# Attention value products: from two split operands over 128 columns to float32, two heads in the halves of the columns

## The chip, the cores and the metric

The kernel runs on one core of one Trainium2 chip. The metric is device time in microseconds for one execution, the median of several runs. Five engines work side by side: TensorE (PE; its weight loads are listed as PEld), VectorE (DVE), ScalarE (ACT), GpSimd (POOL) and SyncE (SP), whose queue issues the DMAs.

## The reference, cut to what matters

One layer of a hybrid encoder: 2064 tokens (16 meta tokens and 2048 others) of width 1024. After a projection, 8 heads of width 64 do stick-breaking attention over causal key prefixes, a recurrent branch (RG-LRU) runs beside it, an output projection and a gated FFN with a causal convolution follow. What the change touches is the attention:

```
for blk in range(t_len // Q_BLOCK):            # 128 queries
    z = einsum("bhqd,bhkd->bhqk", qb, kb) * scale
    mask = s_pos < t_pos
    log_keep = where(mask, log_sigmoid(-z), 0.0)
    after = cumsum(log_keep, reverse=True) - log_keep
    w = where(mask, exp(log_sigmoid(z) + after), 0.0)
    out = einsum("bhqk,bhkd->bhqd", w, vb)
```

The kernel uses the same thing in another form. With S the product of sigmoid(-z) from a key to the end, a weight is a difference of two neighbouring S, so the output is the last value plus a sum of S times the differences of neighbouring value rows.

## The kernel before, in words

The kernel works in stages. First come the norm, the projections and the recurrent branch (to some 580 us), then attention, then the output projection with the second norm (from some 1126 us), then the FFN. Products that must be as exact as float32 are made from operands in a shorter format (float32r): an operand is split into a high part H (a cast) and a low part L (the rest), and H·H, H·L and L·H are added.

Attention goes by head (8) and, within a head, by groups g of two query blocks of 128 (8 groups, and g = -1 for the meta tokens), in the order 3, 7, -1, 0, 6, 1, 5, 2, 4. There are 72 such units. The products of one unit are issued ahead of the outputs of the unit before it (`late`). The order on each engine is then set by a planner that simulates the program and issues by its own costs; the trace shows what it chose.

`load_head` (lines 115 to 144) brings a head's keys (`K2`: H and L in the two halves of the partitions) and two shifted copies of its values; GpSimd subtracts them (line 136) and splits the difference into H and L (lines 92, 93), which lie side by side in `dv`, 64 + 64 columns. Two sets of these buffers alternate between heads. `load_q` (line 548) brings the queries of a unit, four buffers.

`products_of` (555): for one query block, a float32r matmul with the queries' H and one with their L for each chunk of up to 512 keys (569, 570), the sigmoid on ScalarE (571), then a scan on VectorE backwards over the keys (578 for the first chunk with the mask, 580 for two chunks at a time). The result `kp` has 128 queries by all keys of the prefix.

`outputs_of` (616) transposes `kp` by 128x128 blocks on TensorE (helper on line 97) into a PSUM bank of 512 columns, that is two key blocks by two query blocks. When a bank is full, `flush` (600) empties it: ScalarE casts it to float32r (`tH`, line 585, by turns into the tiles `qk` and `tH`), VectorE subtracts (`tL`, 586), and for each key block two matmuls run (612), with all 128 columns of `dv` as the stationary operand and the 256 columns of `tH` and then `tL` as the moving one. So all four partial products H·H, H·L, L·H, L·L are formed; the two halves of the accumulator's partitions hold those with the high and those with the low part of `dv`. There is one accumulator bank `v`. `store_o` (588) adds the last value as a bias on ScalarE (594), and stores both halves apart (596). The output projection's `mix` (521) loads both and adds them on VectorE (526), and loads the recurrent branch.

Of the kernel before, what the change touches and what calls it, by code (L numbers as in the profile page):

```python
# [16 lines left out]
P = 128  # L17
# [21 lines left out]
def f(ap):  # L39
    return ap.bitcast(F32)  # L40
# [15 lines left out]
def hymba_block(  # L56
# [22 lines left out]
    od = {g: dram.tile([2, 4, P, META if g < 0 else 2 * P], F32, name=f"od{g + 1}") for g in range(-1, NT // 2)}  # L79
# [32 lines left out]
    heads = {}  # L112
    hb_stack = ExitStack()

    def load_head(hd, hb):
        j, hh = hd // 2, hd % 2
        rows = slice(hh * HD, hh * HD + HD)
        K2 = hb.tile([P, T], F32R, name="K2", tag="K2")
        dv = hb.tile([P, NT + 1, 2, HD], F32R, name="dv", tag="dv")
        nc.gpsimd.memset(f(dv[:, NT]), 0.0)  # L120
        cuts = [0, 4, 8, NT]
        for s0, s1 in zip(cuts, cuts[1:]):
            c0 = s0 * P + (META if s0 else 0)
            c1 = s1 * P + META
            for e in range(2):
                nc.sync.dma_start(f(K2[e * HD:(e + 1) * HD, c0:c1]), kd[j][e, rows, c0:c1])
            va = hb.tile([P, 9, HD], F32, name="va", tag="va")
            vb = hb.tile([P, 9, HD], F32, name="vb", tag="vb")
            m = s1 - s0
            for v, o in ((va, 1), (vb, 0)):  # L130
                nc.sync.dma_start(v[:, :m], vd[j][o + s0 * P:o + s1 * P, hh].rearrange("(s p) d -> p s d", p=P))
                if s1 == NT:
                    nc.sync.dma_start(v[:META, m], vd[j][o + NT * P:o + T, hh])
            parts = [(P, u, u + 4) for u in range(0, m, 4)] + ([(META, m, m + 1)] if s1 == NT else [])
# [4 lines left out]
        vl = hb.tile([NT + 1, HD], F32, name="vl", tag="vl")  # L139
        nc.sync.dma_start(vl[0:1], vd[j][META:META + 1, hh])  # L140
        nc.sync.dma_start(vl[1:], vd[j][META + P:1 + T:P, hh])
        vlT = hb.tile([P, NT + 1], F32, name="vlT", tag="vlT")
        nc.gpsimd.memset(vlT[HD:], 0.0)
        return j, rows, K2, dv, vlT, vl

# [23 lines left out]
    with ExitStack() as A:  # L169
# [332 lines left out]
        def before(j, i):  # L502
            if j == 2 and i == 0:
                heads[0] = load_head(0, hbE)
# [16 lines left out]
    def mix(mH, mL, src, t0, n):  # L521

        g, c0 = (-1, 0) if t0 < META else divmod(t0 - META, 2 * P)
# [3 lines left out]
        for ks, m in ((slice(0, 4), src[0]), (slice(4, 8), src[2])):  # L527
            nc.scalar.copy(mH[:, ks], m)
            nc.vector.tensor_tensor(mL[:, ks], m, f(mH[:, ks]), op=ALU.subtract)
# [4 lines left out]
    with ExitStack() as B:  # L534
# [10 lines left out]
        G = 2  # L545
        LOW = META + 8 * P

        def load_q(head, t0, n):
            j, rows = head[:2]
            q2 = hq.tile([P, 2, G * P], F32R, name="q2", tag="q2", bufs=4)  # L550
            for e in range(2):
                nc.sync.dma_start(f(q2[e * HD:(e + 1) * HD, :, :n]), qd[j][:, rows, t0:t0 + n].rearrange("s d t -> d s t"))
            return q2

        def products_of(head, i, q2, qc):

            K2 = head[2]
# [8 lines left out]
            for ci, sz in enumerate(sizes):  # L566
                c0 = hi - sz if ci == 0 else c0 - sz
                zt = acc_bank()
                nc.tensor.matmul(zt[:rn, :sz], lhsT=q2[:, 0, qc:qc + rn], rhs=K2[:, c0:c0 + sz], start=True, stop=False)  # L569
                nc.tensor.matmul(zt[:rn, :sz], lhsT=q2[:, 1, qc:qc + rn], rhs=K2[:, c0:c0 + sz], start=False, stop=True)  # L570
# [13 lines left out]
        def evac(h, l, src):  # L584
            nc.scalar.copy(h, src)
            nc.vector.tensor_tensor(l, src, f(h), op=ALU.subtract)  # L586

        def store_o(head, av, i0, t0, m):
            j, rows, vlT = head[0], head[1], head[4]
            ov = a1.tile([P, G * P], F32, name="qn", tag="qn", bufs=2)  # L590
            for c in range(0, m, P):
                e = min(c + P, m)
                b = i0 + 1 + c // P
                nc.scalar.activation(ov[:, c:e], av[:, c:e], AF.Identity, bias=vlT[:, b:b + 1])
            for a in range(2):
                nc.sync.dma_start(od[i0 // G][a, j, rows, :m], ov[a * HD:(a + 1) * HD, :m])

        nflush = [0]

        def flush(head, av, pend, cols, pt, nj):  # L600
            dv = head[3]
            nflush[0] += 1
            if nflush[0] % 2:
                tH = a1.tile([P, 2, 256], F32R, name="qk", tag="qk", bufs=2).rearrange("p a t -> p (a t)")
            else:
                tH = wk.tile([P, 512], F32R, name="tH", tag="tH", bufs=2)
            tL = wk.tile([P, 512], F32R, name="tL", tag="tL", bufs=4)
            pp = pend[0][2]
# [7 lines left out]
        def outputs_of(head, g, kps):  # L616
            if g < 0:
                pt = tu_bank()
                transpose(pt[:META, :META], kps[0][:META, :META])
                av = pmv.tile([P, 2, 256], F32, name="v", tag="v")[:, 0]  # L620
                flush(head, av, [(0, 0, META, 0, META)], META, pt, 1)
                store_o(head, av, -1, 0, META)
                return
            i0 = g * G
            av = pmv.tile([P, 2, 256], F32, name="v", tag="v")[:, 0]
            nj = i0 + G + 1
            pend, cols = [], 0
            pt = tu_bank()
            for s in range(nj):
                first = max(0, s - 1 - i0)  # L630
                nn = (G - first) * P
                if cols + nn > 512:
                    flush(head, av, pend, cols, pt, nj)
                    pt = tu_bank()
                    pend, cols = [], 0
                for b in range(first, G):
                    c = cols + (b - first) * P
                    transpose(pt[:, c:c + P], kps[b][:, s * P:(s + 1) * P])
                pend.append((s, first * P, P, cols, nn))
                cols += nn  # L640
            flush(head, av, pend, cols, pt, nj)
            store_o(head, av, i0, META + i0 * P, G * P)

        def make_products(head, g):
            if g < 0:
                return [products_of(head, -1, load_q(head, 0, META), 0)]
            q2 = load_q(head, META + g * G * P, G * P)
            return [products_of(head, g * G + b, q2, b * P) for b in range(G)]
# [3 lines left out]


        def finish_head(head):

            vlT, vl = head[4:]
            pt = tu_bank()
            transpose(pt[:HD, :NT + 1], vl)
            nc.vector.tensor_copy(vlT[:HD], pt[:HD, :NT + 1])

        units = [(hd, g) for hd in range(HEADS) for g in (3, 7, -1, 0, 6, 1, 5, 2, 4)]
        late = []
        seen = set()
        for n, (hd, g) in enumerate(units):
            if hd not in heads:
                heads[hd] = load_head(hd, (hbE, hbO)[hd % 2])
            if hd not in seen:
                seen.add(hd)
                finish_head(heads[hd])
            if late:  # L670
                outputs_of(*late.pop(0))
            kps = make_products(heads[hd], g)
            late.append((heads[hd], g, kps))
# [17 lines left out]
        tabs = [staging(), staging(), wl.tile([P, LOW + 112], F32, name="kp", tag="kp", bufs=4)[:, :512]]  # L691
# [41 lines left out]
    with ExitStack() as CD:  # L733
# [24 lines left out]
        with ExitStack() as C:  # L758
# [8 lines left out]
            def mixed(i):  # L767
                src = [cp.tile([P, 4, P], F32, name=f"m{a}", tag=f"m{a}", bufs=1) for a in range(3)]
                mix(*(mA, mB)[i % 2], src, META + (i - 1) * P, P)
# [244 lines left out]
```

## Time and profile before

| | us |
|---|---|
| three runs | 2718.18, 2722.47, 2722.88 |
| median | 2722.47 |
| the profiled execution | 2722.01 |
| its span in the trace | 2720.3 |
| TensorE busy | 2563.3 (94%) |
| VectorE busy | 1802.9 (66%) |
| ScalarE busy | 1241.5 (46%) |
| GpSimd busy | 1185.4 (44%) |

All trace numbers come from one profiled execution. The trace's times run from the start of its span. A busy TensorE is no sign that it is at its peak: its products overlap, and their ends are modelled. A share over the whole span mixes stages with different limits, so the views below are taken by stretch.

### The profile page before, as it was taken

Reading aid. Unit: us, or ns where it says so; the run is one execution under the profiler, and the core shown is the slowest. Engines: PE = TensorE matmul, PEld = TensorE weight load, DVE = VectorE, ACT = ScalarE, POOL = GpSimd, SP = SyncE. Lnnn points to the kernel's source line nnn. Section 1 sums busy time; section 2 is a strip of 40 time slices with the busy share of each in tenths; the row PEclk is TensorE's granted clock in tenths of the full one; section 3 lists DMA queues with packets and bytes.
Section 4 is the critical chain, followed back from the end, with each engine's and each line's share of the span. In section 5 each row is a group of like instructions: output and inputs, shape, how many; then the busy total and the mean of one; then the engine's idle time right before and its main releaser. Section 6 shows DMA issues by size and latency. Waiting matters only on the chain. (4 is left out here: it accounts for less than half of the span.)

```text
span 2720.3 us, 40399 instructions
## 1 busy us (share of the span) xinstructions
PE 2563.3 (94%) x15012; PEld 2293.5 (84%) x15012; DVE 1802.9 (66%) x2080; ACT 1241.5 (46%) x2331; POOL 1185.4 (44%) x1152
## 2 busy tenths in 40 slices
PE   7998889988888888999899999999999999999999
PEld 6998889977777778788799999988788888887887
DVE  5678853259999999655677667553745666665443
ACT  4355532246666666432355454432434545453221
POOL 4455564434522321000265555534456665653443
PEclk9999989999999999999899999999999999999999
DMA  5311143243333321577322222244653222225463
GB/s 157 111 33 33 45 113 98 76 113 96 102 81 85 83 78 50 138 222 223 108 86 71 91 74 78 86 159 146 208 169 109 79 84 79 85 79 172 141 211 109
DMA packets 316860, 296.41 MB, mean 109 GB/s; under 512 B 62182, under 2 KB 269270, under 8 KB 316662
## 3 DMA queue, kind: packets, MB, share of 16 engines
q1 hardware_dynamic: 316662, 293.82, 35.5%
q8 instruction: 118, 1.93, 0.3%
q14 instruction: 80, 0.66, 0.1%
HBM read 211.68 MB, written 82.07 MB: 108 GB/s over the span
## 5 line engine op out<-in xcount | busy, mean ns | idle before, releaser
L876 PE MATMUL bk<-mb,wt 128*128 128x258 f32 (+2 forms) x5544 | 878.8, 321 | 11.5 <-ACT u L906 2.3
L876 PEld LDWEIGHTS bk<-mb,wt 128*128 128x128 f32 x5544 | 794.9, 190 | 95.4 <-DVE c L910 3.2
L705 POOL TENSOR_TENSOR wt<-wst,wt 128x512 fp32r<-128x512 f32 (+1 forms) x264 | 485.5, 1845 | 488.8 <-ACT wt L704 263.6
L705 DVE TENSOR_TENSOR wt<-t,wt 128x512 fp32r<-128x512 f32 x88 | 173.4, 1973 | 213.0 <-ACT wt L704 213.0
L108 PE MATMUL bk<-wt 128*128 128x512 f32 x704 | 276.4, 394 | 8.0 <-ACT wt L704 8.0
L109 PE MATMUL bk<-wt 128*128 128x512 f32 x704 | 276.6, 393 | 0.0
L110 PE MATMUL bk<-wt 128*128 128x512 f32 x704 | 271.9, 391 | 4.2 <-DVE wt L705 4.2
L704 ACT CAST wt<-wst 128x512 fp32r<-128x512 f32 (+1 forms) x264 | 200.1, 762 | 121.3 <-PE bk L876 111.8
L705 POOL TENSOR_TENSOR wt<-ss,wt 128x512 fp32r<-128x512 f32 x132 | 197.0, 1495 | 121.7 <-ACT wt L704 120.4
L580 DVE TENSOR_TENSOR_SCAN kp<-kp 128x456 f32<-128x456 f32 (+6 forms) x144 | 238.2, 1655 | 0.9
L612 PE MATMUL v<-tL,dv 128*128 128x256 f32 (+1 forms) x648 | 178.7, 300 | 43.5 <-DVE tL L586 42.4
L938 DVE SCALAR_TENSOR_TENSOR t<-c,fw,t 128x1024 f32<-128x1024 f32 x88 | 135.1, 1535 | 116.0 <-ACT t L937 116.0
L571 ACT ACTIVATE kp<-m 128x388 f32<-128x388 f32 (+13 forms) x360 | 169.0, 508 | 70.7 <-PE m L570 39.7
L704 ACT CAST wt<-t 128x512 fp32r<-128x512 f32 x88 | 54.6, 621 | 281.2 <-PE bk L110 231.4
L612 PEld LDWEIGHTS v<-tL,dv 128*128 128x128 f32 x648 | 125.6, 194 | 59.1 <-DVE tL L586 57.4
L108 PEld LDWEIGHTS bk<-wt 128*128 128x128 f32 x704 | 133.9, 190 | 37.0 <-ACT wt L704 9.0
L110 PEld LDWEIGHTS bk<-wt 128*128 128x128 f32 x704 | 132.8, 189 | 33.0 <-DVE wt L705 5.5
L109 PEld LDWEIGHTS bk<-wt 128*128 128x128 f32 x704 | 133.9, 190 | 27.9
L940 DVE SCALAR_TENSOR_TENSOR c<-c,fw,t 128x1024 f32<-128x1024 f32 x88 | 154.0, 1750 | 3.0
L563 POOL MEMSET kp<- 128x112 f32 x128 | 23.7, 190 | 285.0 <-PE t L97 130.9
L569 PE MATMUL m<-K,q 128*128 128x452 f32 (+12 forms) x360 | 143.2, 399 | 2.5 <-ACT kp L571 2.2
L578 DVE TENSOR_TENSOR_SCAN kp<-kp,mask 128x388 f32<-128x388 f32 (+15 forms) x136 | 130.3, 968 | 0.1
(300 smaller groups left out, 5508.1 us busy)
## 6 DMA issues: line engine op xcount, KB each, us to landing
wst<-in_w_ffn_in_dram SPq DMA_DIRECT2D x88, 512.0 KB, 4.1
wst<-in_w_ffn_out_dram SPq DMA_DIRECT2D x88, 512.0 KB, 5.4
pd<-c SPq DMA_DIRECT2D x44, 512.0 KB, 3.3
t<-pd SPq DMA_DIRECT2D x88, 256.0 KB, 3.5
q<-qd SPq DMA_DIRECT2D x128, 128.0 KB, 2.8
wst<-in_w_in_dram SPq DMA_DIRECT2D x48, 192.0 KB, 2.8
xt<-in_x_dram SPq DMA_DIRECT2D x16, 512.0 KB
od<-qn SPq DMA_DIRECT2D x128, 64.0 KB, 2.1
```

Of the source, the lines that this page charges most:

```text
L108: nc.tensor.matmul(ps, lhsT=sH, rhs=mH, start=first, stop=False)
L109: nc.tensor.matmul(ps, lhsT=sH, rhs=mL, start=False, stop=False)
L110: nc.tensor.matmul(ps, lhsT=sL, rhs=mH, start=False, stop=last)
L569: nc.tensor.matmul(zt[:rn, :sz], lhsT=q2[:, 0, qc:qc + rn], rhs=K2[:, c0:c0 + sz], start=True, stop=False)
L571: nc.scalar.activation(kp[:rn, c0:c0 + sz], zt[:rn, :sz], AF.Sigmoid, scale=-0.125)
L580: nc.vector.tensor_tensor_scan(rev, rev, rev, initial=kp[:rn, hi:hi + 1], op0=ALU.mult, op1=ALU.bypass)
L612: nc.tensor.matmul(av[:, q0:q0 + nn], lhsT=dv[:pp, s].rearrange("p a d -> p (a d)"), rhs=tt[:pp, c:c + nn], start=(s == 0 and half == 0), ...
L704: nc.scalar.copy(h, src)
L705: low.tensor_tensor(l, src, f(h), op=ALU.subtract)
L876: nc.tensor.matmul(ps_, lhsT=s, rhs=m, start=first and k == 0 and n_ == 0, stop=k == 3 and n_ == 2, skip_group_check=True)
L938: nc.vector.scalar_tensor_tensor(t, c_[:, HALO - 1:HALO - 1 + PHW], pf[:, 1:2], t, op0=ALU.mult, op1=ALU.add)
L940: nc.vector.scalar_tensor_tensor(c_[:, uv], c_[:, uv], pf[:, 0:1], t, op0=ALU.mult, op1=ALU.add)
```

## The change

The unit of attention becomes one query block of a pair of heads (4 pairs, 17 blocks each, 68 units) in place of two query blocks of one head. `load_pair` loads both heads' keys and one array of value differences, which stay float32 and are not split. The weights' transposes are copied out of PSUM once, to float32 (by ScalarE, and for the second head in every fifth flush by VectorE), with no high and low part. For each key block there are then two matmuls in float32, one for each head: 64 columns of the stationary operand, 128 of the moving one, with the output in partitions 0 to 63 for the first head and 64 to 127 for the second. The accumulator then holds the two heads' outputs, not two halves of one sum, so it is emptied and stored once, and `mix` loads one array and adds nothing. Score products, sigmoids, scans and transposes keep their number and shape. A pair is loaded during the pair before it, ahead of its unit 13, not at its own start.

```diff
@@ output buffers and load_head @@
-    od = {g: dram.tile([2, 4, P, META if g < 0 else 2 * P], F32, name=f"od{g + 1}") for g in range(-1, NT // 2)}
+    od = [dram.tile([4, P, META if i < 0 else P], F32, name=f"od{i + 1}") for i in range(-1, NT)]
-    def load_head(hd, hb):
-        K2 = hb.tile([P, T], F32R, name="K2", tag="K2")
-        dv = hb.tile([P, NT + 1, 2, HD], F32R, name="dv", tag="dv")
+    def load_pair(j, hb):
+        K2 = [hb.tile([P, T], F32R, name=f"K2{e}", tag=f"K2{e}") for e in range(2)]
+        dv = hb.tile([P, NT + 1, 2, HD], F32, name="dv", tag="dv")
...
-                nc.sync.dma_start(f(K2[e * HD:(e + 1) * HD, c0:c1]), kd[j][e, rows, c0:c1])
+                for a in range(2):
+                    nc.sync.dma_start(f(K2[e][a * HD:(a + 1) * HD, c0:c1]), kd[j][a, e * HD:(e + 1) * HD, c0:c1])
...
-            for n, u0, u1 in parts:
-                nc.gpsimd.tensor_tensor(vb[:n, u0:u1], vb[:n, u0:u1], va[:n, u0:u1], op=ALU.subtract)
-                split_pool(dv[:n, s0 + u0:s0 + u1, 0], dv[:n, s0 + u0:s0 + u1, 1], vb[:n, u0:u1])
+            for u in range(s0, s1, 4):
+                va = a1.tile([P, 4, 2, HD], F32, name="vt", tag="vt", bufs=2)
+                for v, o in ((va, 1), (dv[:, u:u + 4], 0)):
+                    nc.sync.dma_start(v, vd[j][o + u * P:o + (u + 4) * P].rearrange("(s p) h d -> p s h d", p=P))
+                nc.gpsimd.tensor_tensor(dv[:, u:u + 4], dv[:, u:u + 4], va, op=ALU.subtract)
...
@@ mix @@
-        for a, d in enumerate((od[g][0, :, :, c0:c0 + n], od[g][1, :, :, c0:c0 + n], old[:, :, t0:t0 + n])):
+        for a, d in enumerate((od[-(-t0 // P)], old[:, :, t0:t0 + n])):
             nc.sync.dma_start(src[a], d.rearrange("k p t -> p k t"))
-        nc.vector.tensor_tensor(src[0], src[0], src[1], op=ALU.add)
@@ load_q: for each head of the pair @@
-        q2 = hq.tile([P, 2, G * P], F32R, name="q2", tag="q2", bufs=4)
+        q2 = (hq, wk)[e].tile([P, 2, P], F32R, name="q2", tag="q2", bufs=4)[:, :, :n]
@@ flush @@
-            evac(tH[:pp, :cols], tL[:pp, :cols], pt[:pp, :cols])
-            for s, q0, pp, c, nn in pend:
-                for half, tt in enumerate((tH, tL)):
-                    nc.tensor.matmul(
-                        av[:, q0:q0 + nn], lhsT=dv[:pp, s].rearrange("p a d -> p (a d)"), rhs=tt[:pp, c:c + nn],
-                        start=(s == 0 and half == 0), stop=(s == nj - 1 and half == 1))
+            for e in range(2):
+                if nflush[0] % 2:
+                    tT = f(a1.tile([P, 2, 256], F32R, name="qk", tag="qk", bufs=2).rearrange("p a t -> p (a t)"))
+                else:
+                    tT = wk.tile([P, 512], F32, name="tT", tag="tT", bufs=4)
+                if e and nflush[0] % 5 == 1:
+                    nc.vector.tensor_copy(tT[:pp, :cols], pts[e][:pp, :cols])
+                else:
+                    nc.scalar.copy(tT[:pp, :cols], pts[e][:pp, :cols])
+                ts.append(tT)
+            for s, nn in pend:
+                c = s % 4 * P
+                for e in range(2):
+                    nc.tensor.matmul(
+                        av[e * HD:(e + 1) * HD], lhsT=dv[:pp, s, e], rhs=ts[e][:pp, c:c + nn],
+                        start=s == 0, stop=s == nj - 1)
@@ outputs_of: four key blocks at a time, a bank for each head @@
+            for s0 in range(0, nj, 4):
+                blocks = range(s0, min(s0 + 4, nj))
+                pts = [tu_bank() for e in range(2)]
+                for e in range(2):
+                    for s in blocks:
+                        transpose(pts[e][:n, (s - s0) * P:(s - s0) * P + n], kps[e][:n, s * P:s * P + n])
+                flush(pair, av, [(s, n) for s in blocks], n, pts, nj)
+            ov = a1.tile([P, 256], F32, name="qn", tag="qn", bufs=2)
+            nc.scalar.activation(ov[:, :n], av, AF.Identity, bias=vlT[:, i + 1:i + 2])
+            nc.sync.dma_start(od[i + 1][j], ov[:, :n])
@@ the loop @@
-        units = [(hd, g) for hd in range(HEADS) for g in (3, 7, -1, 0, 6, 1, 5, 2, 4)]
+        order = (7, 15, -1, 0, 14, 1, 13, 2, 12, 3, 11, 4, 10, 5, 9, 6, 8)
+        units = [(j, g) for j in range(4) for g in order]
...
+            if g == 13 and j < 3:
+                pairs[j + 1] = load_pair(j + 1, (hbO, hbE)[j % 2])
```

## Rows read from the trace of the kernel before

**Rows 1.** Stretch, length, busy PE, PEld, DVE, ACT, POOL (instructions), PE clock, DMA share, GB/s.
```profile
583.00:1120.00 537.00, 458.62 (x3195) 413.54 (x3194) 534.33 (x655) 354.83 (x852) 170.52 (x271) 0.97 0.33 84
583.00:600.00 17.00, 10.97 (x57) 8.19 (x57) 17.00 (x18) 10.79 (x28) 7.73 (x9) 0.95 0.64 169
...
1133.00:1320.00 187.00, 187.00 (x887) 155.64 (x886) 93.68 (x134) 51.38 (x86) 13.40 (x32) 1.00 0.68 206
```

**Rows 2.** DVE in the same stretch, lines 586, 578, 580 in turn.
```profile
583.00:1120.00 537.00, 194.75 (x353) 0.97 0.33 84
...
583.00:1120.00 537.00, 130.28 (x136) 0.97 0.33 84
...
583.00:1120.00 537.00, 238.24 (x144) 0.97 0.33 84
```

**Rows 3.** Waits from 600 to 1126 us: total, times, longest.
```profile
PE v L612 <- DVE tL L586: 42.4, 47, 5.0
...
PE u L97 <- DVE tL L586: 23.6, 23, 2.4
...
SPq L596 <- ACT kp L571: 52.6, 25, 7.5
```

**Rows 4.** Spacing: FFN windows (257 and 512 columns; columns as rows 1), transposes on the timeline.
```profile
1500.00:1600.00 100.00, 100.00 (x840) 100.00 (x839) 69.33 (x75) 49.07 (x90) 54.76 (x45) 1.00 0.25 80
...
2520.00:2680.00 160.00, 160.00 (x707) 132.54 (x706) 68.80 (x38) 47.14 (x60) 71.89 (x30) 1.00 0.53 173
...
801.81 1.05 PE L97 MATMUL t<-ident,kp 128*128 128x128 f32 x8
...
802.88 0.62 PE L97 MATMUL u<-ident,kp 128*128 128x128 f32 x4
```

**Rows 5.** The value products by tile: ns min/median/max, first and last start, forms.
```profile
L612 PE MATMUL v<-tL,dv x648: 221/281/580, 601.8 to 1126.1; 128*128 128x256 f32 x144, 128*128 128x128 f32 x16, 16*128 16x16 f32 x2
...
L612 PE MATMUL v<-qk,dv x324: 218/280/562, 599.4 to 1125.8; 128*128 128x256 f32 x144, 128*128 128x128 f32 x16, 16*128 16x16 f32 x2
```

**Rows 6.** DVE in the output projection by line: copy out of PSUM, sum of halves.
```profile
L812 DVE COPY sT<-u x17: 215/683/693, 1149.3 to 1327.8; 128x512 f32<-128x512 f32 x16, 128x64 f32<-128x64 f32 x1
...
L526 DVE TENSOR_TENSOR m<-m,m x15: 684/691/693, 1136.1 to 1287.4; 128x512 f32<-128x512 f32 x15
```

**Rows 7.** Scans beside a quiet GpSimd (900 to 920 us) and a busy one (680 to 700).
```profile
900.00:920.00 20.00, 18.07 (x128) 16.14 (x129) 20.00 (x25) 13.77 (x33) 2.38 (x5) 1.00 0.35 86
...
680.00:700.00 20.00, 16.57 (x117) 15.02 (x116) 19.80 (x23) 12.33 (x30) 19.70 (x22) 0.93 0.54 147
...
L578 DVE TENSOR_TENSOR_SCAN kp<-kp,mask 128x456 f32<-128x456 f32 x1 | 1.1, 1090 | 0.0
...
L578 DVE TENSOR_TENSOR_SCAN kp<-kp,mask 128x474 f32<-128x474 f32 x1 | 1.9, 1859 | 0.0
```

**Rows 8.** ScalarE from 583 to 1120 us, lines 585, 571, 594 in turn.
```profile
583.00:1120.00 537.00, 179.74 (x354) 0.97 0.33 84
...
583.00:1120.00 537.00, 167.79 (x358) 0.97 0.33 84
...
583.00:1120.00 537.00, 41.35 (x132) 0.97 0.33 84
```

**Rows 9.** Timeline at 1127 us: products and loads with 48, 16, 128 stationary columns.
```profile
1127.17 0.40 PE L103 MATMUL pu<-woH,mM 128*48 128x512 f32 x1
1127.41 0.40 PE L105 MATMUL pu<-woL,mM 128*16 128x512 f32 x1
...
1133.38 0.39 PE L103 MATMUL pu<-woH,mM 128*48 128x512 f32 x1
1133.61 0.39 PE L108 MATMUL pu<-woH,mB 128*128 128x512 f32 x1
...
1127.41 0.12 PEld L103 LDWEIGHTS pu<-woH,mM 128*48 128x48 f32 x1
```

**Rows 10.** DMA issues: count, size, median us to landing.
```profile
q<-qd SPq DMA_DIRECT2D x128, 128.0 KB, 2.8
```

More of the change, by code (lines that the diff above doesn't have):

```diff
@@ L110, in mm3 @@
         nc.tensor.matmul(ps, lhsT=sL, rhs=mH, start=False, stop=last)
-    heads = {}
+    pairs = {}
     hb_stack = ExitStack()
-    def load_head(hd, hb):
-        j, hh = hd // 2, hd % 2
-        rows = slice(hh * HD, hh * HD + HD)
-        K2 = hb.tile([P, T], F32R, name="K2", tag="K2")
-        dv = hb.tile([P, NT + 1, 2, HD], F32R, name="dv", tag="dv")
-        nc.gpsimd.memset(f(dv[:, NT]), 0.0)
+    def load_pair(j, hb):
+        K2 = [hb.tile([P, T], F32R, name=f"K2{e}", tag=f"K2{e}") for e in range(2)]
+        dv = hb.tile([P, NT + 1, 2, HD], F32, name="dv", tag="dv")
+        nc.gpsimd.memset(dv[:, NT], 0.0)
         cuts = [0, 4, 8, NT]
@@ L125, in load_head @@
             for e in range(2):
-                nc.sync.dma_start(f(K2[e * HD:(e + 1) * HD, c0:c1]), kd[j][e, rows, c0:c1])
-            va = hb.tile([P, 9, HD], F32, name="va", tag="va")
-            vb = hb.tile([P, 9, HD], F32, name="vb", tag="vb")
+                for a in range(2):
+                    nc.sync.dma_start(f(K2[e][a * HD:(a + 1) * HD, c0:c1]), kd[j][a, e * HD:(e + 1) * HD, c0:c1])
             m = s1 - s0
[L130 to L134, printed above, removed]
-            for n, u0, u1 in parts:
-                nc.gpsimd.tensor_tensor(vb[:n, u0:u1], vb[:n, u0:u1], va[:n, u0:u1], op=ALU.subtract)
-                split_pool(dv[:n, s0 + u0:s0 + u1, 0], dv[:n, s0 + u0:s0 + u1, 1], vb[:n, u0:u1])
-        vl = hb.tile([NT + 1, HD], F32, name="vl", tag="vl")
-        nc.sync.dma_start(vl[0:1], vd[j][META:META + 1, hh])
-        nc.sync.dma_start(vl[1:], vd[j][META + P:1 + T:P, hh])
+            for u in range(s0, s1, 4):
[3 more added lines that the diff above has]
+                nc.gpsimd.tensor_tensor(dv[:, u:u + 4], dv[:, u:u + 4], va, op=ALU.subtract)
+        va = a1.tile([P, 4, 2, HD], F32, name="vt", tag="vt", bufs=2)
+        for v, o in ((va[:META, 0], 1), (dv[:META, NT], 0)):
+            nc.sync.dma_start(v, vd[j][o + NT * P:o + T])
+        nc.gpsimd.tensor_tensor(dv[:META, NT], dv[:META, NT], va[:META, 0], op=ALU.subtract)
+        vl = hb.tile([NT + 1, P], F32, name="vl", tag="vl")
+        nc.sync.dma_start(vl[0:1], vd[j][META:META + 1].rearrange("o h d -> o (h d)"))
+        nc.sync.dma_start(vl[1:], vd[j][META + P:1 + T:P].rearrange("o h d -> o (h d)"))
         vlT = hb.tile([P, NT + 1], F32, name="vlT", tag="vlT")
-        nc.gpsimd.memset(vlT[HD:], 0.0)
-        return j, rows, K2, dv, vlT, vl
+        return j, K2, dv, vlT, vl
     ps_mv = ExitStack()
@@ L503, in before @@
             if j == 2 and i == 0:
-                heads[0] = load_head(0, hbE)
+                pairs[0] = load_pair(0, hbE)
         qkv_run([1, 2, 3], w, before, None, A.close)
@@ L521, in mix @@
     def mix(mH, mL, src, t0, n):
[L523 to L524 removed]
+        for a, d in enumerate((od[-(-t0 // P)], old[:, :, t0:t0 + n])):
             nc.sync.dma_start(src[a], d.rearrange("k p t -> p k t"))
[L526 to L527 removed]
+        for ks, m in ((slice(0, 4), src[0]), (slice(4, 8), src[1])):
             nc.scalar.copy(mH[:, ks], m)
@@ L544, in hymba_block, with load_q, products_of @@
         )
-        G = 2
         LOW = META + 8 * P
-        def load_q(head, t0, n):
-            j, rows = head[:2]
-            q2 = hq.tile([P, 2, G * P], F32R, name="q2", tag="q2", bufs=4)
-            for e in range(2):
-                nc.sync.dma_start(f(q2[e * HD:(e + 1) * HD, :, :n]), qd[j][:, rows, t0:t0 + n].rearrange("s d t -> d s t"))
-            return q2
-        def products_of(head, i, q2, qc):
-            K2 = head[2]
+        def load_q(pair, e, t0, n):
+            j = pair[0]
+            q2 = (hq, wk)[e].tile([P, 2, P], F32R, name="q2", tag="q2", bufs=4)[:, :, :n]
+            for a in range(2):
+                nc.sync.dma_start(
+                    f(q2[a * HD:(a + 1) * HD]), qd[j][:, e * HD:(e + 1) * HD, t0:t0 + n].rearrange("s d t -> d s t"))
+            return q2
+        def products_of(K2, i, q2):
             rn, t0 = (META, 0) if i < 0 else (P, META + i * P)
@@ L568, in products_of @@
                 zt = acc_bank()
-                nc.tensor.matmul(zt[:rn, :sz], lhsT=q2[:, 0, qc:qc + rn], rhs=K2[:, c0:c0 + sz], start=True, stop=False)
-                nc.tensor.matmul(zt[:rn, :sz], lhsT=q2[:, 1, qc:qc + rn], rhs=K2[:, c0:c0 + sz], start=False, stop=True)
+                nc.tensor.matmul(zt[:rn, :sz], lhsT=q2[:, 0], rhs=K2[:, c0:c0 + sz], start=True, stop=False)
+                nc.tensor.matmul(zt[:rn, :sz], lhsT=q2[:, 1], rhs=K2[:, c0:c0 + sz], start=False, stop=True)
                 nc.scalar.activation(kp[:rn, c0:c0 + sz], zt[:rn, :sz], AF.Sigmoid, scale=-0.125)
@@ L582, in products_of @@
             return kp
[L584 to L596, printed above, removed]
@@ L598, in hymba_block, with flush @@
         nflush = [0]
-        def flush(head, av, pend, cols, pt, nj):
-            dv = head[3]
+        def flush(pair, av, pend, pp, pts, nj):
+            dv = pair[2]
             nflush[0] += 1
[L603 to L608, printed above, removed]
-            evac(tH[:pp, :cols], tL[:pp, :cols], pt[:pp, :cols])
-            for s, q0, pp, c, nn in pend:
-                for half, tt in enumerate((tH, tL)):
-                    nc.tensor.matmul(
-                        av[:, q0:q0 + nn], lhsT=dv[:pp, s].rearrange("p a d -> p (a d)"), rhs=tt[:pp, c:c + nn],
-                        start=(s == 0 and half == 0), stop=(s == nj - 1 and half == 1))
@@ L616, in outputs_of @@
[L616 to L648, printed above, removed]
+            cols = sum(nn for s, nn in pend)
+            ts = []
+            for e in range(2):
[8 more added lines that the diff above has]
+                ts.append(tT)
@@ new lines, in flush, with outputs_of @@
+            for s, nn in pend:
+                c = s % 4 * P
+                for e in range(2):
+                    nc.tensor.matmul(
+                        av[e * HD:(e + 1) * HD], lhsT=dv[:pp, s, e], rhs=ts[e][:pp, c:c + nn],
+                        start=s == 0, stop=s == nj - 1)
+        def outputs_of(pair, i, kps):
+            j, vlT = pair[0], pair[3]
+            n, nj = (META, 1) if i < 0 else (P, i + 2)
+            av = pmv.tile([P, 512], F32, name="v", tag="v")[:, :n]
+            for s0 in range(0, nj, 4):
[8 more added lines that the diff above has]
+            nc.sync.dma_start(od[i + 1][j], ov[:, :n])
@@ L650, in staging, with make_products, finish_pair @@
+        def make_products(pair, i):
+            t0, n = (0, META) if i < 0 else (META + i * P, P)
+            return [products_of(pair[1][e], i, load_q(pair, e, t0, n)) for e in range(2)]
         def staging():
             return a1.tile([P, 4, 2, HD], F32, name="vt", tag="vt", bufs=2).rearrange("p a b d -> p (a b d)")
-        def finish_head(head):
-            vlT, vl = head[4:]
+        def finish_pair(pair):
+            vlT, vl = pair[3:]
             pt = tu_bank()
-            transpose(pt[:HD, :NT + 1], vl)
-            nc.vector.tensor_copy(vlT[:HD], pt[:HD, :NT + 1])
@@ L661, in hymba_block @@
-        units = [(hd, g) for hd in range(HEADS) for g in (3, 7, -1, 0, 6, 1, 5, 2, 4)]
+            transpose(pt[:, :NT + 1], vl)
+            nc.vector.tensor_copy(vlT, pt[:, :NT + 1])
+        order = (7, 15, -1, 0, 14, 1, 13, 2, 12, 3, 11, 4, 10, 5, 9, 6, 8)
+        units = [(j, g) for j in range(4) for g in order]
         late = []
[L663 to L669, printed above, removed]
+        for n, (j, g) in enumerate(units):
+            if g == order[0]:
+                finish_pair(pairs[j])
@@ L670, in hymba_block @@
             if late:
                 outputs_of(*late.pop(0))
-            kps = make_products(heads[hd], g)
-            late.append((heads[hd], g, kps))
+            if g == 13 and j < 3:
+                pairs[j + 1] = load_pair(j + 1, (hbO, hbE)[j % 2])
+            kps = make_products(pairs[j], g)
+            late.append((pairs[j], g, kps))
             k = n - (len(units) - 2 * KD)
@@ L689, in hymba_block @@
                     split_pool(woH[:, k, es], woL[:, k, es], st)
-        tabs = [staging(), staging(), wl.tile([P, LOW + 112], F32, name="kp", tag="kp", bufs=4)[:, :512]]
+        tabs = [staging(), staging()]
         mix(mM[:, :, 0], mM[:, :, 2], [t[:, :4 * META].rearrange("p (k t) -> p k t", k=4) for t in tabs], 0, META)
@@ L767, in mixed @@
             def mixed(i):
-                src = [cp.tile([P, 4, P], F32, name=f"m{a}", tag=f"m{a}", bufs=1) for a in range(3)]
+                src = [cp.tile([P, 4, P], F32, name=f"m{a}", tag=f"m{a}", bufs=1) for a in range(2)]
                 mix(*(mA, mB)[i % 2], src, META + (i - 1) * P, P)
```

## Prediction

> **What bounds the kernel now.** I read the busy time by stretch first. From 583 to 1120 us, the attention stage, VectorE (DVE) is busy 534 of 537 us, TensorE 459, ScalarE 355 and GpSimd 171 [rows 1]. In the output projection after it TensorE is the full one, 187 of 187 us [rows 1]. So this stage has an owner other than TensorE. The groups of DVE work in it come next: the two scans (lines 578 and 580) take 130.3 and 238.2 us, the subtraction that makes the low half of the transposed weights (line 586) 194.8 us [rows 2]. These add to 563 against a union of 534, because neighbours overlap by some 5%; I scale by 0.95. Then the waits: TensorE's lines 612 and 97 stand still for that subtraction 42.4 + 23.6 = 66 us [rows 3], of its 537 - 459 = 78 us idle. The subtraction is therefore on the path twice over: it fills the bounding engine and it is the releaser.
>
> What TensorE needs in the stage is less than its busy time, since modelled ends overlap. I price by spacing. The FFN runs without a gap: 840 products of on average 257 columns in 100 us are 0.119 us each, 707 of 512 columns in 160 us 0.2263 [rows 4]; so 0.42 ns per column and 0.011 us per instruction. Transposes: eight in a row take 1.05 us, four 0.62, so 0.1075 each [rows 4]. The stage holds 720 score products over 2 x 8 x 17,680 = 282,880 columns (16 for the meta block, 16 + 128(i+1) for block i): 127 us. Transposes: 153 per head, 1224 in all: 132 us. Value products: 648 with the low part, 324 with each of the two tiles of the high part, 1296 [rows 5], of which 1152 have 256 columns (0.119 us) and nearly all others 128 (some 0.11): 151 us. Sum 410 us, 76% of the stage.
>
> **The change, part by part.** *DVE.* All 360 subtractions go: 195 x 0.95 = 185 us. Of the 360 copies out of PSUM that stay, the second head's in every fifth flush goes to DVE: 180 flushes, 36 copies; a DVE copy of 512 columns out of PSUM takes 0.683 us [rows 6], together at most 24 us. The scans don't change. 534 - 185 + 24 = 373 us. GpSimd's work on value differences falls from three passes to one (the two splits go), and it costs DVE: a scan of 474 columns took 1.86 us in a stretch with GpSimd 98% busy, one of 456 columns 1.09 us where it was 12% busy [rows 7]. I put 10 us to that: DVE 363.
>
> *ScalarE.* Copies 180 us, sigmoids 168, exits of the accumulator 41 [rows 8]. A tenth of the copies leaves (18), and the exits halve, one for both heads (20). By the union, 355 - 38 = 317 us: not the bound.
>
> *TensorE.* Scores and transposes keep number and shape: 127 + 132 = 259 us. The value products become, for each pair of heads and key block, one float32 product per head, 64 columns of stationary against 128 of moving: 4 x 153 = 612 pairs of instructions. No row of the trace has a float32 product other than a transpose, nor two products in different halves of the array's columns, so I bound the pair. From below: a transpose, one pass of float32 over 128 columns, costs 0.1075 [rows 4]; with both heads at once a pair costs that, 66 us in all. From above: the 1296 products replaced form four partial products (high and low of each operand) of 64 columns each, side by side in 128. If a float32 product does the same four in turn, it streams 4 x 128 = 512 columns, 0.2263 by the row of that width [rows 4], and if the second head then waits for the first, a pair costs 0.4526, 277 us. I take 0.2263: four passes, because as much arithmetic is asked as now, and the halves at the same time, because they use different columns and different accumulator partitions; this second half is the choice on which all hangs, and rows give it no proof. 612 x 0.2263 = 139 us; TensorE 398 us. The weight loads hide: 48 columns load in 0.12 us behind a product of 0.23 [rows 9].
>
> The Trainium skill ("FP8 and Floating Point Precision", section TensorE Precision Notes) gives true float32 four passes through the array; by it a head's product is 512 columns and the sum would be the same 398 us with the halves together, 536 in turn.
>
> *What ends the stage.* TensorE 398 against DVE 363: TensorE is late next, DVE close behind. Its idle time lies between 12 us (78 now less the 66 that wait for the subtraction; 6 of it stands in the first 17 us, where it waits for the first scans [rows 1]) and the 78 of now. One accumulator bank, an in-order ScalarE that serves sigmoids and copies, and DVE 90% full all leave waits, so I take 40, near the middle. 398 + 40 = 438 us, 99 less than 537.
>
> *Costed at nothing.* Queries come in twice as many loads of half the width, and outputs in one store for two; the DMA engines are 33% busy in the stage [rows 1], and a query load lands in 2.8 us [rows 10], with four buffers for each head. Stores on SP's queue wait for ScalarE, 53 us at one releaser alone [rows 3], and the loads stand behind them; 68 stores in place of 144 make that less. Loads of the next pair's keys and values are issued with ten units of the pair still to come, where a head's were issued at its own start; they pass SP's query loads and GpSimd's memsets, and the waits name no product that waited for keys. If that cover fails, it costs a few landings of such a load at three changes of pair, some 10 us each by 2.8 apiece. In the output projection the sum of halves goes (15 x 0.69 us of DVE [rows 6]), beside a TensorE that is full for 187 us [rows 1]: nothing.
>
> The sum: the profiled execution took 2722.0 us with a span of 2720.3; 2722 - 99 = 2623. The median of the three runs is 2722.5, so the two agree. I say 2625.
>
> **Rivals.** *The second head waits for the first (slower).* Half the array then idles in every value product. TensorE needs 259 + 277 = 536 us, what the whole stage takes today; it has lost DVE as its brake and gained as much work. DVE at 363 no longer disturbs it, so idle is 12 to 40, say 20: 556, or 2741 (2733 to 2761). With 40 idle the change breaks even at a pair price of (537 - 40 - 259) / 612 = 0.389 us; the mechanism decides from there up. For it: no row shows two products at once, and the widths of 16 and 48 that appear get no discount, 0.23 us each [rows 9]. Against it: those all sit in the same first columns, so they show nothing on separate halves.
>
> *Overlap, but paid for at each change of width.* A full-width product or transpose may have to wait until the halves have run empty, and the other way round. A change then exposes what a 256-column product lasts beyond its spacing, 0.28 - 0.12 = 0.16 us [rows 5]; two changes for each of 180 flushes are 58 us. 398 + 58 + 40 = 496: 2681. About the same comes out when only parts of the four passes overlap (0.34 a pair: 467 + 30 = 497). Band 2661 to 2725. Against it: where products with 48, 16 and 128 stationary columns follow each other they start 0.23 us apart, as in a uniform run [rows 9].
>
> The Trainium skill ("TensorEngine Tiling (Array Packing)", Overview and Key Properties) says that tiles operate independently, up to twice as fast for 64 columns, but also that a change of tiling mode drains the engine. The first supports the forecast, the second is this rival; the trace agrees with the drain nowhere, as the changes between 48, 16 and 128 columns cost nothing visible, but no row has a tile in the upper half.
>
> How low it can go: DVE at 373 us without the 10 for GpSimd is still below TensorE's 398, so TensorE sets the floor; with 12 us of idle 410, or 2595.
>
> **How the numbers follow.** Halves together: 0.66 (2595 to 2661). Overlap with a price: 0.14. In turn: 0.20. Faster by over 0.2% (about what a measurement of this kernel can tell from no change, 5.4 us): the first two, 0.80. Within: 0.03, slower: 0.17, both from the last case. The range: from 2595, the little idle, through the first two cases; with some of the first outside its bounds these hold under 0.8, so it reaches into the third, to 2738. The likeliest case's own range is 2595 to 2661.
>
> **What would show it.** In the attention stage of the changed kernel: DVE busy 350 to 380 us; the stage some 440 us long; line 705 and the others of the FFN as before. The value products of the two heads should start nearly together, with a pair every 0.23 us; a pair every 0.45 means in turn. Gaps of 0.1 to 0.2 us at the first value product or transpose after the other kind mean the price of a change. If DVE still stands at 99% of a shorter stage, the split of the copies is what I have mis-sized. The prediction is wrong if the pair costs over 0.3 us, or if TensorE's idle time stays near 78 us with another releaser.

## The result and the profile after

The changed kernel takes 2662.32 us (median of four runs, 2660.23 to 2664.19) against 2721.44 for the kernel before in the same comparison: a ratio of 0.9784 (95% interval 0.9772 to 0.9796). The profiled execution took 2664.2 us with a span of 2662.4, 57.9 us less than before. The time lies 1 us above the band of the case that the forecast held likeliest (2595 to 2661) and at the lower edge of the band of the second rival, overlap that is paid for at each change of width. It is inside the stated range, 2595 to 2738, which was drawn over the rivals too.

All of it is in the attention stage. The first product of the output projection starts at 1067.5 us (second line), and at 1126.3 before (first line): 59 us.

```profile
1126.25 0.39 PE L103 MATMUL pu<-woH,mM 128*48 128x512 f32 x1
...
1067.53 0.43 PE L103 MATMUL pu<-woH,mM 128*48 128x512 f32 x1
```

Busy time by stretch in the changed kernel (columns as in [rows 1]): attention, a stretch with GpSimd at work, four microseconds of it, and the output projection.

```profile
583.00:1068.00 485.00, 466.38 (x4397) 392.75 (x4396) 383.20 (x332) 325.89 (x757) 99.41 (x171) 0.99 0.32 83
...
840.00:920.00 80.00, 72.36 (x663) 61.06 (x662) 76.23 (x53) 50.69 (x119) 60.29 (x60) 0.96 0.38 110
880.00:884.00 4.00, 2.90 (x12) 2.72 (x12) 4.00 (x4) 1.46 (x3) 3.83 (x4) 0.57 0.41 127
...
1080.00:1260.00 180.00, 180.00 (x857) 150.02 (x856) 81.86 (x114) 48.21 (x81) 12.71 (x32) 1.00 0.60 182
```

VectorE was busy 534 of 537 us [rows 1] and is now busy 383 of 485; TensorE has 466 of 485. The owner of the stage has changed. VectorE's groups in the stage (count, busy, mean ns, idle before and what ended it):

```profile
L574 DVE TENSOR_TENSOR_SCAN kp<-kp 128x694 f32<-128x694 f32 (+11 forms) x144 | 236.5, 1645 | 43.2 <-ACT kp L565 35.2
L572 DVE TENSOR_TENSOR_SCAN kp<-kp,mask 128x388 f32<-128x388 f32 (+15 forms) x136 | 130.8, 976 | 30.5 <-ACT kp L565 30.4
```

The scans cost what they did [rows 2], and now VectorE waits for the sigmoids ahead of them. TensorE's waits that the trace records were 66 us for the subtraction alone [rows 3]; now they are some 20 us in all, and these are the four largest (total, times, longest):

```profile
PE t L97 <- DVE tT L592: 4.9, 2, 3.2
PE t L97 <- DVE kp L574: 4.7, 4, 2.7
PE u L97 <- DVE kp L574: 2.8, 2, 2.3
PE m L563 <- DMA q<-qd: 2.8, 1, 2.8
```

The value products by tile, where [rows 5] had 1296 in all, and two pieces of TensorE's timeline (start, length, engine, line; xN is the number of records in a row):

```profile
L599 PE MATMUL v<-qk,dv x1224: 204/273/324, 594.5 to 1066.9; 128*64 128x128 f32 x174, 16*64 16x16 f32 x1
...
L599 PE MATMUL v<-tT,dv x1224: 204/273/472, 600.3 to 1067.3; 128*64 128x128 f32 x173, 16*64 16x16 f32 x2
...
801.30 1.09 PE L599 MATMUL v<-tT,dv 128*64 128x128 f32 x16
802.22 1.04 PE L599 MATMUL v<-qk,dv 128*64 128x128 f32 x16
803.10 1.04 PE L599 MATMUL v<-tT,dv 128*64 128x128 f32 x16
804.07 0.98 PE L97 MATMUL u<-ident,kp 128*128 128x128 f32 x7
...
889.14 0.43 PE L599 MATMUL v<-qk,dv 128*64 128x128 f32 x2
889.51 0.66 PE L97 MATMUL u<-ident,kp 128*128 128x128 f32 x4
```

There are 2448 records for 1224 products: a float32 product is two loads and two matmuls in the trace. Sixteen records are eight products, four pairs, and the second sixteen start 0.88 us before the third: 0.22 us a pair. In the single records the two heads' matmuls start 5 to 7 ns apart, and the next two 0.109 us after the first two, so a pair is 0.218 us. From the third sixteen to the transposes behind them, though, 0.97 us pass, and from the first, which follow transposes, to the second 0.92, not 0.88.

The two lines at 889 us show something else: one head's product alone, with other work before and behind it. By the single records, 54 of the 167 unbroken groups of value products are such a product, and 50 of the 612 pairs run one head after the other.

### The profile page after: what moved, and what is told of

It reads as the page before. It is cut to its first block, busy times and chain, and to the rows that moved or that the text cites. A ratio compares the mean times of both kernels' runs of the same rounds, so it can differ in the third digit from the quotient of the medians.

```text
span 2662.4 us, 41934 instructions
## 1 busy us (share of the span) xinstructions
PE 2565.2 (96%) x16160; PEld 2267.7 (85%) x16160; DVE 1638.7 (62%) x1735; ACT 1208.8 (45%) x2227; POOL 1108.3 (42%) x1040
## 5 line engine op out<-in xcount | busy, mean ns | idle before, releaser
L574 DVE TENSOR_TENSOR_SCAN kp<-kp 128x694 f32<-128x694 f32 (+11 forms) x144 | 236.5, 1645 | 43.2 <-ACT kp L565 35.2
L565 ACT ACTIVATE kp<-m 128x412 f32<-128x412 f32 (+11 forms) x360 | 160.2, 507 | 34.6 <-PE m L564 31.4
L563 PE MATMUL m<-K,q 128*128 128x412 f32 (+11 forms) x360 | 136.5, 383 | 4.8 <-DMA q<-qd 2.8
L564 PE MATMUL m<-K,q 128*128 128x412 f32 (+11 forms) x360 | 124.7, 350 | 0.0
L675 ACT CAST wt<-ss 128x512 fp32r<-128x512 f32 x132 | 81.9, 622 | 82.8 <-PE bk L847 73.3
```

What stands on the lines that cost most here:

```text
L563: nc.tensor.matmul(zt[:rn, :sz], lhsT=q2[:, 0], rhs=K2[:, c0:c0 + sz], start=True, stop=False)
L565: nc.scalar.activation(kp[:rn, c0:c0 + sz], zt[:rn, :sz], AF.Sigmoid, scale=-0.125)
L574: nc.vector.tensor_tensor_scan(rev, rev, rev, initial=kp[:rn, hi:hi + 1], op0=ALU.mult, op1=ALU.bypass)
```

## The experiments

The runs fell in three comparisons, each with the kernel before beside it (2724.97, 2721.72, 2723.93 us). Differences to the changed kernel are taken by way of it: the changed kernel is 59.1 us faster than the one beside it, and 61.4 in its second showing below. The first four experiments are one execution each; executions of the changed kernel lie between 2657 and 2665, so their times are good to some 5 us.

The theory after the result: the halves of the columns do overlap, every change between half and full width costs TensorE some 0.1 us, and the rest of the stage is arithmetic and waits. Its rivals: the halves run in turn and a float32 product is simply cheap; a change of width is free and the gaps have another cause; VectorE was not what bounded the kernel before.

**Both heads in the same half.**

```diff
-                        av[e * HD:(e + 1) * HD], lhsT=dv[:pp, s, e], rhs=ts[e][:pp, c:c + nn],
+                        av[:HD, e * P:e * P + nn], lhsT=dv[:pp, s, e], rhs=ts[e][:pp, c:c + nn],
...
```

> The changed kernel, but both heads' float32 products go to the same half of the columns (partitions 0 to 63 of the accumulator, the second head 128 columns further on). Theory: the two halves overlap in the changed kernel, so here a pair of products costs 0.436 us in place of 0.218; 612 x 0.218 = 133 us more: about 2795 us. Rival: the halves run in turn already, and a float32 product of 128 columns simply costs two steps of 0.055 us; then the time stays at 2662, but for some 10 us for the accumulator's exits in two pieces.

Measured: 2777.96 us, 53 slower than before, so 112 more than the changed kernel. Its timeline:

```profile
802.33 1.96 PE L599 MATMUL v<-qk,dv 128*64 128x128 f32 x16
804.13 1.91 PE L599 MATMUL v<-tT,dv 128*64 128x128 f32 x16
```

Sixteen records after other work now take 1.80 us in place of 0.92. The value products have the same widths and the same number of columns, and only the place of their output differs; besides, the accumulator is emptied and stored in two pieces. The spacing of the products themselves shows the overlap. Of the 133 us expected, 112 came. The 133 take all 612 pairs to run together in the changed kernel; the 562 that do make 123, and the rest was not followed up.

**Full width.**

```diff
-                        av[e * HD:(e + 1) * HD], lhsT=dv[:pp, s, e], rhs=ts[e][:pp, c:c + nn],
+                        av[:, e * P:e * P + nn], lhsT=dv[:pp, s].rearrange("p a d -> p (a d)"), rhs=ts[e][:pp, c:c + nn],
...
```

> The changed kernel, but each float32 product uses all 128 columns of the value differences of both heads (half of its output is not used), so that no product has another width than the transposes and scores around it. Theory: the halves overlap, and each change between half and full width costs TensorE some 0.12 us, 333 of them 40 us; then this one has the doubled products (133 us) without the changes: 40 us less than the kernel with both heads in the same half, about 2755. Rival: a change of width is free and TensorE's gaps have another cause; then it equals the kernel with both heads in the same half, about 2795.

Measured: 2748.95 us, 29.0 less than with both heads in the same half. Both run the products in turn, 1.79 us for sixteen records here:

```profile
804.12 1.95 PE L599 MATMUL v<-qk,dv 128*128 128x128 f32 x16
805.91 0.27 PE L97 MATMUL u<-ident,kp 128*128 128x128 f32 x1
```

What is missing is the price of the changes, to which the comparison of the two times points. The median step from the start of the last instruction of one kind to the start of the first of the next, in us, worked out from all starts of the stage in each trace (count in brackets):

| from, to | changed kernel | same half | full width |
|---|---|---|---|
| value product, transpose | 0.203 (144) | 0.203 (139) | 0.112 (135) |
| transpose, value product | 0.203 (104) | 0.202 (87) | 0.109 (91) |
| score, value product | 0.282 (63) | 0.291 (73) | 0.204 (73) |
| value product, score | 0.202 (22) | 0.202 (20) | 0.031 (28) |

Every change costs 0.08 to 0.09 us more than the same step at full width, and 0.17 where a score product follows. By these counts the changed kernel pays 144 x 0.091 + 104 x 0.094 + 63 x 0.078 + 22 x 0.171 = 32 us, and the comparison of the two kernels says 29.

That agreement is in part an accident, since two terms stand outside the count. Behind a change to half width, the first two matmuls of a head's product start 0.160 us apart, where later ones start 0.109 apart: so in 162 of the 167 groups of the changed kernel, and in 15 of 164 at full width. That is 0.05 us more a group, 8 us. On the other side, a full-width record takes 0.112 us where a half-width one takes 0.109, some 6 us over the stage. So the changes cost the changed kernel some 40 us.

**More changes.**

```diff
+                if len(pend) > 2 and s == pend[1][0]:
+                    nc.tensor.matmul(
+                        full[:, 256:272], lhsT=pair[1][0][:, :P], rhs=pair[1][0][:, :16],
+                        start=False, stop=False, skip_group_check=True)
...
```

> The changed kernel with one more product of full width and 16 columns, its result not used, in the middle of every group of value products that has three or four key blocks: 144 times, so 288 more changes of width. Theory: a change costs some 0.12 us, so 35 us more and some 4 for the products themselves: about 2700. Rival: changes are free: 2662 to 2668.

Measured: 2708.16 us, 16.8 faster than before, so 42 more than the changed kernel. The groups of value products rise from 167 to 309. One of them:

```profile
802.73 0.66 PE L599 MATMUL v<-tT,dv 128*64 128x128 f32 x8
803.32 0.28 PE L603 MATMUL v<-K 128*128 128x16 f32 x1
803.52 0.66 PE L599 MATMUL v<-tT,dv 128*64 128x128 f32 x8
```

Eight records should take 0.44 us; the full-width product starts after 0.59, and the next value product 0.20 later, for 16 columns. The median steps to and from the added product are 0.203 and 0.207 us, where 0.109 would pass without it: 0.30 us for each of 144, and 0.05 more in the first step behind it. The product's own 16 columns are a small part of that. By the starts this is 50 us, and 42 show in the time: the stage had waits that took up some of it. So a change has a price, and most of it lies on the path.

**The kernel before without the subtraction.**

```diff
-            evac(tH[:pp, :cols], tL[:pp, :cols], pt[:pp, :cols])
+            nc.scalar.copy(tH[:pp, :cols], pt[:pp, :cols])
...
-                for half, tt in enumerate((tH, tL)):
+                for half, tt in enumerate((tH, tH)):
```

> The kernel before without the subtractions that make the low part of the transposed weights; the high part is multiplied twice, so TensorE has the same products and VectorE 185 us less (the low part of the weights is left out of the result). Theory: VectorE is the bound of the attention stage before, and TensorE, at 410 us, is late next; the stage falls from 537 to 410 plus 40 to 50 of waits: some 75 to 85 us less, about 2640, below the changed kernel's 2662, since it pays no changes of width. Rival: TensorE or its chain is the bound and VectorE only busy beside it: under 20 us less, above 2700.

Measured: 2632.15 us, 93 less than the kernel before, 34 less than the changed kernel. Its result leaves out the low part of the weights, so it is a bound and no kernel to use. Its attention stage (columns as in [rows 1]):

```profile
583.00:1036.00 453.00, 428.71 (x3233) 410.06 (x3234) 372.49 (x299) 346.52 (x852) 165.89 (x269) 0.98 0.39 98
```

VectorE was the bound: with nothing else touched the stage falls to 453 us, TensorE's 410 by my count plus 43. And VectorE's relief alone is worth more than the whole change. The changed kernel gives about 34 us of it back: some 40 for the changes of width, less 7 that its value products save (144 us as they ran, as worked out below, against the 151 of the prediction's count).

**Longer groups of value products.** Transposes and copies of eight key blocks are issued ahead of the products of all eight.

```diff
-            for s0 in range(0, nj, 4):
...
+            for g0 in range(0, nj, 8):
+                pend = []
+                for s0 in range(g0, min(g0 + 8, nj), 4):
...
+                    ts = evacuate(n, len(blocks) * n, pts)
+                    pend += [(s, ts) for s in blocks]
```

> The changed kernel with the transposes and copies of eight key blocks issued before the value products of all eight, in place of four and four. Theory: some 330 changes of width cost 0.09 to 0.17 us each, 32 us; with fewer and longer groups of value products (some 200 changes) 12 us go: about 2650. Rival: TensorE then waits longer for the copies, since all four transposing banks are taken at once: 2662 or above.

Measured: 2658.77 us (2657.51 to 2663.49; ratio to before 0.9771, 0.9756 to 0.9785). The trace shows 176 groups of value products, where the changed kernel has 167: the planner's order on TensorE undid the edit, so nothing follows on the changes. A second try issued the products of the later four blocks first, so that all eight had to come together:

```diff
+                pend = sorted(pend, key=lambda q: -(q[0] // 4))
...
```

> The kernel with groups of eight key blocks left the order on TensorE as it was (the planner still runs the first four blocks' products as soon as their copies are there), so it made no fewer changes of width. Here the products of the second four blocks are issued first, so that all eight must come together; TensorE should show some 110 groups of value products in place of 167. Theory: 57 groups less, two changes each at 0.1 us, 11 us: about 2650. Rival: the first four blocks' products now wait for the second four's copies, and what the changes give is lost to waits: 2660 or above.

Measured: 2664.33 us (2660.95 to 2665.28; ratio 0.9778, 0.9764 to 0.9793), with 159 groups, not 110: transposes and scores still come between. Both tries failed as edits. Whether fewer changes can be had for less than they save stays open.

**The output projection's weights in pieces.** GpSimd splits them in one stretch, 855 to 912 us, where VectorE is at 95% and TensorE waits (the row of 840 to 920 above).

```diff
-            if k >= 0 and k % 2 == 0:
...
+            if 8 <= n < 8 + 4 * KD:
+                k, es = (n - 8) // 4, slice((n - 8) % 4 * 256, (n - 8) % 4 * 256 + 256)
+                st = a1.tile([P, 256], F32, name="qn", tag="qn", bufs=2)
```

> The changed kernel with the output projection's weights split by GpSimd in pieces of 256 columns, one for each of 32 units, and not in one stretch (855 to 912 us of the changed kernel's trace). Theory: in that stretch GpSimd slows the scans, VectorE becomes the bound for some 60 us and TensorE idles 8 us and then runs a while at the lower clock; spread out, the slowing hides behind TensorE: 8 to 12 us less, about 2652. Rival: it costs nothing there, or the same in pieces: 2660 to 2664.

Measured: 2658.22 us (2653.73 to 2658.82; ratio 0.9766, 0.975 to 0.9783). The same stretch:

```profile
840.00:920.00 80.00, 77.75 (x740) 66.22 (x740) 63.46 (x58) 54.75 (x126) 22.57 (x41) 0.98 0.28 72
```

TensorE has 740 records there in place of 663, and the scans of the stage take 356 us in place of 367. It is 63.5 us faster than before, so 2 to 4 us faster than the changed kernel, under half of what was expected, with an interval that overlaps. The kernel with all copies on ScalarE, below, from which nothing was expected, is 63.8 faster in the same comparison: the time does not show a gain of this edit. With the longer groups as well:

> Both of the edits before at once: groups of eight key blocks, and the output projection's weights split in pieces. Theory: they act on different waits and add: about 2640. Rival: the longer groups take back what the spreading gives: 2650 or above.

Measured: 2656.20 us (2653.47 to 2657.56; ratio 0.9757, 0.9742 to 0.9772), the lowest of these, 65.5 us faster than before, 4 to 6 more than the changed kernel, with intervals that touch, and 1.7 more than the kernel with all copies on ScalarE: no gain is shown here either. With the later blocks first:

> The same, with the output projection's weights split in pieces of 256 columns over 32 units. Theory: 11 us for the changes and 4 for the spreading: about 2646. Rival: 2656 or above, as the kernel with groups of eight in the planner's order and the same spreading.

Measured: 2660.65 us (2658.09 to 2666.89; ratio 0.9772, 0.9756 to 0.9789). The regrouping gives nothing that stands out.

**All copies on ScalarE.**

```diff
-                if e and nflush[0] % 5 == 1:
+                if False:
```

> The changed kernel with all copies of transposed weights on ScalarE, the tenth on VectorE undone. Theory: neither engine is the bound any more (VectorE 383 and ScalarE 326 us of 485), so 36 copies more or less move the end by under 5 us either way: 2657 to 2667. Rival: ScalarE's turn of copies and sigmoids is what TensorE waits for, and it gets 22 us longer: 2670 or above; or VectorE still is: 2650 or below.

Measured: 2657.95 us (2656.05 to 2664.33; ratio 0.9769, 0.9753 to 0.9785): no difference that stands out from the changed kernel, as expected of engines that no longer bound the stage.

**The changed kernel once more**, beside the last two:

> The changed kernel itself once more, to have it on the same chip beside the two: 2660 to 2664.

Measured: 2662.53 us (2657.32 to 2664.99; ratio 0.9772, 0.9757 to 0.9786). One run was below the expected band, and two lay up to 1 us above it.

## Why the prediction was right or wrong

Right: VectorE bounded the stage, its subtraction was the releaser, and taking it away makes TensorE late next. The kernel without the subtraction shows it by itself: 93 us, with TensorE busy 429 of 453 us and VectorE 372.

Right: the choice on which all hung. The halves overlap, and a pair costs 0.218 us where 0.2263 was assumed. But 50 pairs were issued apart, and cost 0.436 each, so the products take 144 us in place of 139. With both heads in one half the time is 2778, where the first rival had 2741; it counted no changes of width. Its break-even of 0.389 us a pair was not put to the test, but 0.44 loses clearly.

The Trainium skill ("TensorEngine Tiling (Array Packing)", Key Properties) says that tiles operate independently and that a change of tiling mode drains the engine. The runs agree with the first, by the 5 to 7 ns between the two heads' starts. They show a price at a change, 0.08 to 0.17 us, but not that it is a drain.

Wrong: the step "What ends the stage", where 398 us of TensorE held no term for the changes. That term was priced, at 58 us, and put into a rival with a chance of 0.14, against it the steady 0.23 us of products with 48, 16 and 128 columns [rows 9]. That row did not bear on the question: those products cost nothing to change, and the half-width ones do. What sets them apart (the width, the place, the float32 format or their column tile) was not tried one by one. The size in the rival was too large: 333 changes at 0.08 to 0.17 us, with the longer first step of 162 groups, are some 40 us, not 58 for 360 at 0.16. The sign that the prediction named for it, gaps of 0.1 to 0.2 us at the first product after the other kind, is in the trace. So what came is the case that the forecast gave 0.14, at two thirds of its price, and the time lies on the border of the two cases.

About right, by luck as far as the runs show: the idle time. With 127 us of scores, 132 of transposes, 144 of value products and 40 of changes, 443 of 485 us are explained, and 42 are left, where 40 was taken between bounds of 12 and 78 without a working. Together: 40 more for the changes, 5 for the products, 2 for idle, 47 in all, which is 485 less 438. The recorded waits hold some 20 of the 42. By the starts, it is spread thin: some 20 us within runs of score products, 10 within transposes, 9 from scores to transposes. Where they come from isn't settled; moving the tenth of the copies from VectorE to ScalarE didn't change the time, and spreading GpSimd's work took some 9 us off the stage in the trace, which is of the quickest of four executions, but no clear gain in the time.

Mis-sized: VectorE at 363; it shows 383. The scans' sum is 367.3 us against 368.5 [rows 2], so GpSimd's lighter load gave nothing of the 10 us put to it. The stretch in which GpSimd splits the output projection's weights took it: a scan of 840 elements takes 2.74 us there (840 to 920 us) and 1.97 from 740 to 820 us, and with the weights in pieces the scans fall to 356 us. Neighbours overlap by 3%, not 5 (395 us of groups in a union of 383). VectorE, at 383 of 485 us, doesn't set the end.

Costed at nothing and rightly so: the output projection is full on TensorE as before, and the loads of queries, keys and values show as waits of TensorE only once, for 2.8 us.

## What to carry to other kernels

When one engine is full and another idles for it, price what the idle one will need afterwards from start-to-start steps, not from its busy time: here that gave the floor of the new stage to within the price of an effect that no row had. Two products that fill half the array's columns each can run side by side, but each switch to and from full-width work costs; so put as many of them as possible behind one switch, and look in the trace whether the planner kept them together. Here 50 of 612 pairs ran apart, which cost 11 us of lost overlap besides the changes; what keeping them together would give was not tried. Ask what the removal alone is worth: without the subtraction, and with nothing put in its place, the kernel before would have been some 34 us faster than the changed one. Its result would not be the same, so this is a bound; by the counts above, most of the 34 us is the changes of width.

## What the runs showed of the hardware

A float32 product of 128 columns is two loads and two matmuls in the trace, 0.109 us each at 64 stationary columns and 0.112 at 128, so 0.22 us, close to the 0.2263 of a 512-column product in the shorter format [rows 4].

Matmuls on the two halves of the columns start 5 to 7 ns apart, though the instructions come from one queue, and a pair costs 0.218 us, no more than one product alone.

A change between half-width float32 products and full-width work costs 0.08 to 0.09 us in three of the four directions, and 0.17 from a value product to a score product, which at full width starts only 0.03 us after the last. The first step of a head's product behind the change is 0.160 us in place of 0.109.

A scan of 840 elements takes 2.74 us on VectorE from 840 to 920 us, where GpSimd is busy 60 of 80 us, and 1.97 from 740 to 820 us, where GpSimd is almost idle.

After a wait of 3.16 us for VectorE at 881 us the granted clock stood at 0.57 on average of the four microseconds around it, and score products of 420 columns started 0.35 us apart, where those of 432 columns elsewhere are 0.20 apart: the lower of the clock's two levels, 1.2 GHz, for a moment. It is rare in this stage (0.99 over all).
